# Block of gMLP, mLSTM and a squared-ReLU MLP on one core: the fetches of the second MLP product's row operands go out from GpSimd's queue instead of SyncE's

## The chip, the core and the metric

The kernel runs on one core of a Trainium2 chip. Five engines work side by side, each through its own instruction stream in order: TensorE (PE, matrix products; PEld is its loading of weights), VectorE (DVE), ScalarE (ACT), GpSimd (POOL) and SyncE (SP). Data move by DMA: an engine issues a transfer, goes on, and whoever needs the data waits on a semaphore. SP does nothing but issue transfers. An engine that has to wait before it may issue holds up everything behind that in its stream. The metric is the device time of one execution in microseconds (us).

## The reference, cut to what matters

One decoder block over 512 tokens of 2048 features, in float32. Two token mixers (a gated MLP with spatial gating and an mLSTM) come first; the part around the change is the MLP behind them and the last norm:

```python
        x = x + mixed @ w_out[l]
        hn = _rms_norm(x, norm2_g[l])
        x = x + jnp.square(jax.nn.relu(hn @ w_ff1[l])) @ w_ff2[l]
    return _rms_norm(x, norm_f_g)
```

`w_ff1` is 2048 x 8192, `w_ff2` 8192 x 2048. "First product" and "second product" below are those two.

## The kernel before, in words

**Precision and form of the products.** Every float32 operand is split into a rounded part hi (ScalarE, a cast) and a rest lo (DVE, a subtraction), and a product is made as three matmuls. The large products use a scheme with seven block products in place of eight: sums and differences of quarters, A11, A12, A22, S1, S2, S3 and S4, stand on both sides, so that operands have to be made from pieces before they can be multiplied.

**First product.** 32 column tiles. `hidden` (L945) applies the squared ReLU and writes each tile to the DRAM tensor `h_d` from POOL (L949).

**Second product.** The 8192 hidden features are worked through in NB = 4 blocks c of 2048, and each in two units, for the column halves j0 = 0 and 4 (`unit`, `token_unit`). A unit has 28 parts of 12 matmuls, four weight chunks for each of the seven operations, in the order A11/S1 in turns, S2/S4 in turns, S3, A12/A22 in turns. Each part needs a weight chunk (512 KB, fetched by SP at L1070 into `raw` or `raw2` buffers), differences of chunks (DVE, L59), and its hi (ACT, L1059) and lo (DVE, L1060). Results are drained from PSUM into tiles `o` (ACT L1160, DVE L1162), and written to the DRAM tensor `sum_d` from POOL (L1167): as plain writes for c = 0, and accumulating for c = 1 and 2. In the last block they come back the other way (L1196).

**The row operands.** What the weights of a unit multiply are the operands h of block c. `hidden_parts(c, ...)` makes them: for each of four groups g, four pieces of `h_d` are fetched by `hidden_piece` (L1020, 128 partitions x 2 x 256 floats, 256 KB each) into `tmp` tiles named hp, and A11, S1, S2 and S4 are made from them; then S3 for each g, from two pieces fetched again; then A12 and A22 for each g, one piece each. That is 32 fetches a block, 128 in all. Each operand costs one sum or difference on DVE (hp, L59; none for A11, A12, A22), a cast on ACT (L137) and a subtraction on DVE (h, L59). The pool `tmp` has four buffers, so a fetch waits until an earlier piece has been used. The operands fill 28 buffers, and a new block's operand waits until the old one in its place has been multiplied for the last time.

**Who runs when.** `hidden_parts` is a generator. `beside` registers it, and each part of a product calls `tick`, which lets every registered generator take one step. The generator for c = 0 starts two ticks into tile 30 of the first product, that for c + 1 in the second unit of block c, when 14 of its 28 parts are done. The framework's scheduler then sets the order on each engine from the order of the code, the dependencies and its own assumed durations, so that one engine's stream mixes both. The weights' hi and lo are held in the order of the parts (`in_turn`). Semaphores follow from the data.

In `before`, SP's stream carries the weight chunks and the fetches of pieces; POOL's carries the writes of `h_d` and `sum_d` and, at the end, of x3.

Of the kernel before, what the change touches and what calls it, by code (L numbers as in the profile page):

```python
# [17 lines left out]
S2 = S // 2  # L18
# [15 lines left out]
def hybrid_block(ctx: ExitStack, tc: tile.TileContext, a: dict, out: bass.AP):  # L34
    nc = tc.nc
# [7 lines left out]
    def t4k(name, dt=F32, shape=None):  # L43
        return sb.tile(shape or [P, 2, S], dt, tag="t4k", bufs=28, name=name)

    def tmp(name, shape=None, dt=F32):
        return sb.tile(shape or [P, S], dt, tag="tmp", bufs=4, name=name)
# [96 lines left out]
    def v2(t):  # L144
        return t.rearrange("p (e t) -> p e t", e=2)
# [641 lines left out]
    def fetch(src, name):  # L787
        t = tmp(name)
        nc.sync.dma_start(t, src)
        return t  # L790
# [67 lines left out]
    for i in range(8):  # L858
        t = t4k(f"mix_{i}")
# [11 lines left out]
    for g in range(4):  # L871
        q = [pair(f"mq_{g}_{kh}") for kh in range(2)]
        for e in range(2):
            for kh in range(2):
# [3 lines left out]
                t = fetch(sg_d[0][j], f"sga_{j}")  # L878
# [62 lines left out]
    h_d = dram.tile([P, DFF // P, S], F32, name="h_d")  # L941
# [78 lines left out]
    def hidden_piece(c, kh, th, g):  # L1020
        t = v2(tmp(f"hp_{c}_{kh}_{th}_{g}"))
        k = c * KT + kh * 8 + g * 2
        nc.sync.dma_start(t, h_d[:, k : k + 2, th * S2 : (th + 1) * S2])
        return t

    def hidden_parts(c, xo):

        for g in range(4):
            a11, a21 = hidden_piece(c, 0, 0, g), hidden_piece(c, 0, 1, g)
            a22, a12 = hidden_piece(c, 1, 1, g), hidden_piece(c, 1, 0, g)  # L1030
            put(xo, "A11", a11, f"h{c}_{g}")
            yield
            put(xo, "S1", tt(a22, a21, a22, ALU.add), f"h{c}_{g}")
            yield
            put(xo, "S2", tt(a22, a22, a11, ALU.subtract), f"h{c}_{g}")
            yield
            put(xo, "S4", tt(a12, a12, a22, ALU.subtract), f"h{c}_{g}")
            yield
        for g in range(4):
            a21, a11 = hidden_piece(c, 0, 1, g), hidden_piece(c, 0, 0, g)  # L1040
            put(xo, "S3", tt(a21, a11, a21, ALU.subtract), f"h{c}_{g}")
            yield
        for g in range(4):
            for op, th in (("A12", 0), ("A22", 1)):
                put(xo, op, hidden_piece(c, 1, th, g), f"h{c}_{g}")
            yield
# [342 lines left out]
```

## Time and profile before

| | before |
|---|---|
| median of 3 runs | 2541.51 us (2537.47 to 2547.2) |
| the profiled execution | 2543.25 us, span 2541.5 us |
| mean granted PE clock | 0.985 of full speed |
| transfers issued by SP (queue q1) | 318.29 MB, 40.3% of the DMA engines' time |
| transfers issued by POOL (queue q0) | 56.71 MB, 7.9% |

The span is the part of the execution in which the profile shows instructions. Times within it count from its start; the second product begins at about 1851 us, and its blocks turn at about 2015, 2177 and 2343 us. The granted clock is the share of TensorE's full speed that the chip allowed over a stretch; its two levels are 1.2 and 2.4 GHz.

### The profile page before, as it was taken

To read this page: it belongs to the slowest core of one execution; us is meant where nothing else is said; L and a number is where in the kernel's file an instruction comes from. 1 tells how busy PE (TensorE), PEld (TensorE's weight loads), DVE (VectorE), ACT (ScalarE), POOL (GpSimd) and SP (SyncE) were. 2 spreads that over 40 slices of the span, in tenths; PEclk is the share of its full clock that TensorE was granted. 3 is DMA by queue.
4 is the path that set the end of the run, shared out by engine and by line. 5 is a ranking of instruction groups with operands and counts; after the bars stand their busy time and mean duration, and the time that the engine had idled before them with its cause. 6 is when DMAs were issued, how large, how long until landed. Compare 5 with 4: busy or idle time off the path is not lost.

```text
span 2541.5 us, 34288 instructions
## 1 busy us (share of the span) xinstructions
PE 2462.9 (97%) x12810; PEld 2080.7 (82%) x12810; DVE 2078.7 (82%) x2852; ACT 1302.1 (51%) x1913; POOL 155.1 (6%) x242
## 2 busy tenths in 40 slices
PE   8999999999999999999999999999989999999996
PEld 7888888888887888888888888888868787787785
DVE  6988888888878756889788888888878878888787
ACT  6555464554455223555555555555654545544544
POOL 0001001001001000000000000000000010011000
PEclk9999999999999999999999999999999999999998
DMA  7323333333335644355344433443665776678564
GB/s 270 109 87 117 124 104 112 121 105 129 112 100 187 206 162 141 110 153 149 103 139 135 137 127 135 134 141 133 212 186 144 237 179 153 181 163 226 144 193 137
DMA packets 197366, 377.17 MB, mean 148 GB/s; under 512 B 14784, under 2 KB 124352, under 8 KB 197200
## 3 DMA queue, kind: packets, MB, share of 16 engines
q1 hardware_dynamic: 177552, 318.29, 40.3%
q0 software_dynamic: 19648, 56.71, 7.9%
q8 instruction: 100, 1.64, 0.3%
q14 instruction: 66, 0.54, 0.1%
HBM read 320.41 MB, written 54.53 MB: 148 GB/s over the span
## 4 chain that ended last, share of the span: by engine, by line
PE 76%; DVE 9%; issue 6%; DMA 6%; ACT 2%; POOL 1%; DVEq 0%; SPq 0%; POOLq 0%; ACTq 0%
PE pw_f_x L155 8%; DMA hp<-h_d 4%; PE pw_f_z L155 4%; PE pw_f_x L156 4%; PE pt_f_x L1092 3%; PE pt_f_x L1090 3%; PE pt_f_x L1091 3%; PE pw_g_x L155 3%; PE pw_f_z L156 2%; PE pw_f_y L155 2%; PE pt_f_z L1092 2%; PE pp_g L155 2%; PE pt_f_z L1090 2%; PE pt_f_z L1091 2%; PE pw_g_x L156 1%
## 5 line engine op out<-in xcount | busy, mean ns | idle before, releaser
L59 DVE TENSOR_TENSOR raw_f<-raw_f,raw_f 128x1024 f32<-128x1024 f32 x228 | 277.5, 1221 | 10.4 <-DMA raw_f<-in_w_ff 8.3
L126 DVE TENSOR_TENSOR lo_f_S<-raw_f,hi_f_S 128x1024 fp32r<-128x1024 f32 x116 | 141.8, 1223 | 44.6 <-ACT hi_f_S L125 44.6
L1059 ACT CAST hi_f_S<-raw_f 128x1024 fp32r<-128x1024 f32 x112 | 116.9, 1048 | 112.7 <-DVE raw_f L59 80.6
L155 PE MATMUL pw_f_z<-x_S,hi_f_S 128*128 128x512 f32 x448 | 163.1, 404 | 0.0
L125 ACT CAST hi_f_A<-raw_f 128x1024 fp32r<-128x1024 f32 x87 | 91.2, 1049 | 137.4 <-DVE raw_f L59 71.6
L155 PE MATMUL pw_f_x<-x_S,hi_f_S 128*128 128x512 f32 x448 | 159.9, 397 | 0.0
L1060 DVE TENSOR_TENSOR lo_f_S<-raw_f,hi_f_S 128x1024 fp32r<-128x1024 f32 x112 | 136.5, 1222 | 28.7 <-ACT hi_f_S L1059 28.2
L155 PE MATMUL pw_f_x<-x_A,hi_f_A 128*128 128x512 f32 x448 | 158.4, 396 | 0.0
L125 ACT CAST hi_f_S<-raw_f 128x1024 fp32r<-128x1024 f32 x116 | 121.2, 1046 | 57.5 <-DVE raw_f L59 30.2
L126 DVE TENSOR_TENSOR lo_f_A<-raw_f,hi_f_A 128x1024 fp32r<-128x1024 f32 x87 | 106.5, 1224 | 46.9 <-ACT hi_f_A L125 46.8
L1059 ACT CAST hi_f_A<-raw_f 128x1024 fp32r<-128x1024 f32 x84 | 87.6, 1046 | 81.4 <-DVE raw_f L59 61.3
L1060 DVE TENSOR_TENSOR lo_f_A<-raw_f,hi_f_A 128x1024 fp32r<-128x1024 f32 x84 | 101.7, 1222 | 33.1 <-ACT hi_f_A L1059 32.8
L156 PE MATMUL pw_f_z<-x_S,lo_f_S 128*128 128x256 f32 x448 | 125.8, 281 | 0.0
L156 PE MATMUL pw_f_x<-x_A,lo_f_A 128*128 128x256 f32 x448 | 125.3, 280 | 0.0
L156 PE MATMUL pw_f_x<-x_S,lo_f_S 128*128 128x256 f32 x448 | 125.3, 280 | 0.0
L1090 PE MATMUL pt_f_x<-hi_f_A,h_A 128*128 128x512 f32 x224 | 91.4, 408 | 17.1 <-ACT hi_f_A L1059 10.3
L155 PEld LDWEIGHTS pw_f_z<-x_S,hi_f_S 128*128 128x128 f32 x448 | 84.8, 189 | 22.8 <-DVE f L59 1.9
L155 PEld LDWEIGHTS pw_f_x<-x_S,hi_f_S 128*128 128x128 f32 x448 | 84.1, 188 | 20.8
L155 PEld LDWEIGHTS pw_f_x<-x_A,hi_f_A 128*128 128x128 f32 x448 | 84.1, 188 | 20.3
L155 PE MATMUL pp_g<-xu,hi_g 128*128 128x512 f32 x256 | 92.7, 406 | 8.1 <-ACT hi_g L125 7.8
L1090 PE MATMUL pt_f_z<-hi_f_S,h_S 128*128 128x512 f32 x224 | 89.3, 398 | 6.6 <-ACT hi_f_S L1059 6.6
L1092 PE MATMUL pt_f_x<-lo_f_A,h_A 128*128 128x512 f32 x224 | 91.3, 409 | 2.6 <-DVE lo_f_A L1060 2.5
(560 smaller groups left out, 7807.6 us busy)
## 6 DMA issues: line engine op xcount, KB each, us to landing
raw_f<-in_w_ff SPq DMA_DIRECT2D x240, 512.0 KB, 4.3
hp<-h_d SPq DMA_DIRECT2D x128, 256.0 KB, 4.2
raw_g<-in_w_gb SPq DMA_DIRECT2D x32, 512.0 KB, 3.9
raw_g<-in_w_ga SPq DMA_DIRECT2D x32, 512.0 KB, 3.3
raw_wout<-in_w_out SPq DMA_DIRECT2D x32, 512.0 KB, 3.3
h_d<-f POOLq DMA_DIRECT2D x60, 256.0 KB, 2.3
sum_d<-o POOLq DMA_DIRECT2D x48, 256.0 KB, 5.8
sg<-g POOLq DMA_DIRECT2D x32, 256.0 KB, 2.4
```

What stands on the lines that cost most here:

```text
L59: V.tensor_tensor(o, x, y, op=op)
L125: in_turn("A", A.copy(hi[:, c], src[:, c]))
L126: in_turn("V", V.tensor_tensor(lo[:, c], src[:, c], hi[:, c].bitcast(F32), op=ALU.subtract))
L155: T.matmul(ps, wh, x, start=first, stop=False, skip_group_check=more)
L156: T.matmul(ps[:, :S2], wl, x[:, :S2], start=False, stop=last, skip_group_check=more)
L1059: in_turn("A", A.copy(vh, v))
L1060: in_turn("V", V.tensor_tensor(vl, v, vh.bitcast(F32), op=ALU.subtract))
L1090: T.matmul(ps[t], xh, wh, start=b, stop=False, skip_group_check=not first)
L1091: T.matmul(ps[t], xl, wh, start=False, stop=False, skip_group_check=not first)
L1092: T.matmul(ps[t], xh, wl, start=False, stop=e, skip_group_check=not first)
```

## The change

One line: the fetch of a piece is issued by GpSimd instead of SyncE.

```diff
     def hidden_piece(c, kh, th, g):
         t = v2(tmp(f"hp_{c}_{kh}_{th}_{g}"))
         k = c * KT + kh * 8 + g * 2
-        nc.sync.dma_start(t, h_d[:, k : k + 2, th * S2 : (th + 1) * S2])
+        nc.gpsimd.dma_start(t, h_d[:, k : k + 2, th * S2 : (th + 1) * S2])
         return t
```

SP's stream goes from 709 rows to 581, POOL's from 240 to 368. The scheduler also sets other orders on ACT and DVE. In the rows below, hp_1_0_3 is the piece kh = 1, th = 0, g = 3 (the number of the block isn't printed), raw_f_0_0_3_0 is block 0, unit 0, quarter 3 of the weights, chunk 0, and operands show only the letter of their operation.

SP at the end of the first product, the difference between the kernel before and the changed one, from the fourth chunk of quarter 1 to the four chunks of quarter 0 with which the first part of the second product begins:

```order
 L1070 DMA raw_f_0_0_3_0_16983<-in_w_ff 128x4x256
-L1023 DMA hp_1_0_3_16750<-h_d 128x2x256
-L1023 DMA hp_0_1_0_16859<-h_d 128x2x256
-L1023 DMA hp_0_0_0_16861<-h_d 128x2x256
-L1023 DMA hp_0_1_1_16887<-h_d 128x2x256
-L1023 DMA hp_0_0_1_16889<-h_d 128x2x256
-L1023 DMA hp_0_1_2_16912<-h_d 128x2x256
-L1023 DMA hp_0_0_2_16914<-h_d 128x2x256
 L1070 DMA raw_f_0_0_0_0_16773<-in_w_ff 128x4x256
 L1070 DMA raw_f_0_0_0_1_16818<-in_w_ff 128x4x256
 L1070 DMA raw_f_0_0_0_2_16867<-in_w_ff 128x4x256
 L1070 DMA raw_f_0_0_0_3_16920<-in_w_ff 128x4x256
```

The seven fetches that stood between the two groups of chunks are gone from SP; the four chunks now follow the one ahead of them directly.

POOL in the turn from block 1 to block 2, of the changed kernel (before, POOL had only the `sum_d` rows here, one behind the other):

```order
L1167 DMA sum_d<-o_4_010_18911 128x512
L1167 DMA sum_d<-o_4_011_18913 128x512
L1023 DMA hp_0_1_3_19189<-h_d 128x2x256
L1023 DMA hp_1_1_3_19191<-h_d 128x2x256
L1023 DMA hp_1_0_3_19193<-h_d 128x2x256
L1023 DMA hp_0_1_0_19298<-h_d 128x2x256
L1167 DMA sum_d<-o_4_110_18769 128x512
L1167 DMA sum_d<-o_4_111_18771 128x512
L1023 DMA hp_0_0_0_19300<-h_d 128x2x256
L1023 DMA hp_0_1_1_19323<-h_d 128x2x256
```

The fetches for S1 of g = 3 (hp_0_1_3 and hp_1_1_3) stand behind the first two writes of sums, and one of the two fetches for the first S3 (hp_0_0_0) behind the next two.

DVE at the same place, the difference: the sum for S1 of g = 3 is the row hp_1_1_3 <- hp_0_1_3, hp_1_1_3, the additions into o are L1162, the operands of the last A12/A22 parts L1060:

```order
 L1060 TENSOR_TENSOR lo_f_1_4_A_0_19036<-raw_f_1_4_2_0_19033,hi_f_1_4_A_0_19035 128x1024
+L59 TENSOR_TENSOR raw_f_1_4_2_0_19033<-raw_f_1_4_2_0_19033,raw_f_1_4_0_0_18617 128x1024
 L59 TENSOR_TENSOR hp_1_1_3_19191<-hp_0_1_3_19189,hp_1_1_3_19191 128x512
-L59 TENSOR_TENSOR raw_f_1_4_2_0_19033<-raw_f_1_4_2_0_19033,raw_f_1_4_0_0_18617 128x1024
-L59 TENSOR_TENSOR h_3_S_19220<-hp_1_1_3_19191,h_3_S_19220 128x2x256
-L59 TENSOR_TENSOR hp_1_1_3_19191<-hp_1_1_3_19191,hp_0_0_3_19187 128x512
 L1162 SCALAR_TENSOR_TENSOR o_4_110_18769<-pt_f_1_4_x_18613,r2c,o_4_110_18769 128x512
 L1162 SCALAR_TENSOR_TENSOR o_4_111_18771<-pt_f_1_4_x_18614,r2c,o_4_111_18771 128x512
 L1060 TENSOR_TENSOR lo_f_1_4_A_0_19057<-raw_f_1_4_2_0_19033,hi_f_1_4_A_0_19056 128x1024
 L1060 TENSOR_TENSOR lo_f_1_4_A_1_19079<-raw_f_1_4_2_1_19076,hi_f_1_4_A_1_19078 128x1024
```

The weight difference raw_f_1_4_2_0 moved ahead of the sum, and the lo half of S1 (h_3_S) and the next difference moved behind the additions into o.

## Rows read from the trace of the kernel before

**Rows 1.** The page: busy time of each engine and two kinds of DMA issues.

```profile
PE 2462.9 (97%) x12810; PEld 2080.7 (82%) x12810; DVE 2078.7 (82%) x2852; ACT 1302.1 (51%) x1913; POOL 155.1 (6%) x242
...
hp<-h_d SPq DMA_DIRECT2D x128, 256.0 KB, 4.2
...
h_d<-f POOLq DMA_DIRECT2D x60, 256.0 KB, 2.3
```

**Rows 2.** Four stretches and a steady one: length, busy time (instructions) by engine, granted clock, DMA.

```profile
1840.00:1880.00 40.00, 28.11 (x111) 21.70 (x110) 32.52 (x40) 24.36 (x36) 1.08 (x2) 0.87 0.64 191
1920.00:1980.00 60.00, 60.00 (x264) 49.19 (x263) 53.58 (x56) 33.55 (x42) 3.13 (x6) 1.00 0.52 142
1980.00:2060.00 80.00, 76.25 (x319) 61.27 (x319) 69.21 (x75) 41.29 (x52) 3.35 (x7) 0.96 0.70 205
2140.00:2200.00 60.00, 52.60 (x207) 41.04 (x206) 49.13 (x57) 27.80 (x36) 6.59 (x8) 0.91 0.82 222
2300.00:2370.00 70.00, 62.45 (x247) 49.44 (x246) 57.89 (x67) 34.01 (x45) 6.91 (x8) 0.90 0.77 206
```

**Rows 3.** PE's waits, 1780 to 2430: waited for, us, times, longest.

```profile
PE pt_f_x L1090 <- ACT hi_f_A L1059: 10.3, 1, 10.3
PE pt_f_x L1090 <- DVE o L1162: 6.8, 3, 2.7
```

**Rows 4.** Timeline of SP, end of the first product: start, us from first to last.

```profile
1832.53 0.37 SPq L1070 DMA_DIRECT2D raw_f<-in_w_ff  x1
1833.13 11.28 SPq L1023 DMA_DIRECT2D hp<-h_d  x7
1844.50 2.47 SPq L1070 DMA_DIRECT2D raw_f<-in_w_ff  x4
```

**Rows 5.** The chain that ended last in 1795 to 1885: start, us, what.

```profile
1844.05 3.07 DMA hp<-h_d
...
1848.86 10.69 DMA hp<-h_d
```

**Rows 6.** Timeline of ACT, 1838 to 1862.

```profile
1846.71 0.35 ACT L162 COPY o_f<-pp_f 128x256 f32<-128x256 f32 x1
...
1850.32 1.04 ACT L1059 CAST hi_f_A<-raw_f 128x1024 fp32r<-128x1024 f32 x1 [1.11 <-DMA raw_f<-in_w_ff]
```

**Rows 7.** The chain in 2144 to 2158, between the second and third block.

```profile
2142.42 7.51 DMA hp<-h_d
...
2149.96 0.69 DVE hp L59
2150.65 1.14 DVE raw_f L59
2151.79 0.61 DVE h_S L59
...
2153.03 1.40 DVE o L1162 x2
```

**Rows 8.** The chain in 2177 to 2192, start of the third block.

```profile
2179.54 7.96 DMA hp<-h_d
...
2189.12 1.24 DVE lo_f_S L1060
```

**Rows 9.** Timeline of POOL, 2130 to 2200.

```profile
2139.69 1.72 POOL L1167 DMA_DIRECT2D sum_d<-o  x2 [43.20 <-DVE o L1162]
2154.07 1.72 POOL L1167 DMA_DIRECT2D sum_d<-o  x2 [12.65 <-DVE o L1162]
2176.61 2.60 POOL L1167 DMA_DIRECT2D sum_d<-o  x3 [20.81 <-DVE o L1162]
```

**Rows 10.** The issues of line 1167: ns min/median/max, then us from issue to landing.

```profile
L1167 POOL DMA_DIRECT2D sum_d<-o x48: 539/850/1408, 1900.7 to 2346.1; - x48
...
DMA to landing us min/median/max: 2.3/5.8/8.6
```

**Rows 11.** The issues of line 1023: ns min/median/max.

```profile
L1023 SPq DMA_DIRECT2D hp<-h_d x128: 359/360/1722, 1796.9 to 2360.4; - x128
```

## The prediction

> **What bounds the kernel now.** I began with the page: TensorE (PE) is busy for 97% of the span, VectorE (DVE) for 82%, and GpSimd (POOL) for only 6% [rows 1]. So only time in which PE stands still or runs slowly can be won, and POOL has room for more issues. The busy time by stretches shows where that time lies. In the steady stretch 264 matmuls take 60.00 us, 0.2273 us each, at full granted clock; in the other four the count of matmuls times 0.2273 us is less than the stretch [rows 2]. The differences are 14.8 us around the start of the second product (40 - 111 x 0.2273), 7.5 us at the turn from block 0 to block 1, 13.0 us from 1 to 2, and 13.9 us from 2 to 3: 49 us together. The granted clock there is 0.87 to 0.96 of 2.4 GHz, thus partly at the lower level of 1.2 GHz, because PE restarts slowly after each pause; that is in the 49 us. All four stretches are those in which the fetches of line 1023 run, so **49 us, 1.9%, is the most that this change can win**.
>
> PE's own waits name two sorts of cause: one wait of 10.3 us for the first rounded weight tile (hi, ScalarE, L1059), and three of together 6.8 us for DVE's additions into o [rows 3]. Next I read what stands ahead of each.
>
> *Start of the second product.* SP's timeline shows one weight chunk issued at 1832.53, then seven fetches over 11.28 us, and only at 1844.50 the four chunks with which the first part begins [rows 4]. A fetch has to wait for one of four tmp buffers, and the weights stand behind it in SP's queue. ScalarE rounds the first chunk at 1850.32, released by its arrival [rows 6]. The chain shows the fetch for the third S3 landing at 1847.12 and the one for the fourth S3 taking 10.69 us, against a median of 4.2 us, since 2 MB of weights were issued just ahead of it [rows 1, 5].
>
> *Turns between blocks.* In the turn from 1 to 2 a fetch issued at 2142.42 lands 7.51 us later, at 2149.93. DVE then does the sum of pieces (0.69 us), a weight difference (1.14 us), the lo half of S1 (0.61 us) and one more difference before the additions into o start at 2153.03; PE's next part waits for those [rows 3, 7]. At the start of block 2 a fetch issued at 2179.54 takes 7.96 us and holds up a cast, so that the lo part of S1's second chunk comes at 2189.12 [rows 8]. The other turns look alike.
>
> **The change, part by part.** The one edited line moves 128 issues from SP to POOL, and the order of ScalarE's and DVE's work follows from it.
>
> *The issue.* An issue on SP takes 0.36 us [rows 11]. No 128-partition fetch on POOL is in the trace; the nearest are the plain writes of the same 256 KB, at 0.54 us [rows 10], landing after a median of 2.3 us [rows 1]. I take 0.54 us and the old time to landing. The 128 issues then cost POOL 69 us on an engine that is 94% idle. Where fetches follow one another through the buffers it costs 0.18 us each. I see no reason why the first byte must come sooner or later; the bounds are 2.3 us (the write) and 7.96 us (the longest that held up a turn).
>
> *Start of the second product.* SP now has the four chunks right behind the one of 1832.53, some 11 us earlier, so they are there before ScalarE wants them (a flight took 5.8 us, 1844.50 to 1850.32). In the new order hi stands behind the cast of the second S3 and the copy at 1846.71 that ends at 1847.06 [rows 6], no longer behind the cast of the third S3. So it can start 3.3 us sooner. Its lo half still stands behind the sum of the third S3 on DVE, and that fetch (1847.12) ends a row of three that each pay 0.18 us and now share the DMA engines with 2 MB of weights. I take **-2 us**, of a possible -3.3, and 0 if the fetches lose as much as the weights gain. The fourth S3's fetch no longer stands behind those weights: with the median of 4.2 us it lands 6.5 us earlier. Of the 14.8 us some 4.5 us are not the one long wait; I take **-2 us** of these, at most -4.5.
>
> *Turns: DVE's order.* The weight difference now stands ahead of the sum that waits, and the lo half of S1 and the second difference behind the additions into o. With an unchanged landing the additions start 0.69 us after it, at 2150.65 instead of 2153.03: 2.4 us for each turn.
>
> *Turns: POOL's queue.* What takes it back is that a fetch now stands behind writes of sums. Those that stand just ahead of it were issued from 2139.69 to 2141.41, so the issue itself isn't held; but they are accumulating, with a median of 5.8 us to landing and up to 8.6 us [rows 9, 10]. They can be underway until 2149.2 (2140.55 + 8.6), with two fetches behind them, while the weights on SP's queue no longer stand ahead. I take a landing 1 us later than now; the bounds are 2 us earlier and 4 us later. In the turn from 0 to 1 the sums are plain writes (0.54 us to issue, 2.3 us at least to landing): no delay taken.
> Two other places are in the same queue. The fetch for the first S3 now stands behind the sums issued at 2154.07, which wait for DVE; before it came ahead of them. I take a new wait of 1 us (bounds 0 and 4) in each of the turns 1 to 2 and 2 to 3. The last fetch for the fourth S3 stands behind the three of 2176.61, so it goes out after 2179.2; with the 7.96 us of now it lands at 2187.2, and lo comes after a sum and a difference (0.69 + 1.14 us), at 2189.0, as now; with 5.8 us it gains 2 us. I take -1 us.
>
> So 0 to 1: -2.4 and a little of slow clock, **-3 us**. 1 to 2 and 2 to 3: -2.4 + 1 + 1 - 1 = -1.4, **-1.5 us** each.
>
> **The sum** is -2 - 2 - 3 - 1.5 - 1.5 = -10 us. The profiled execution took 2543.25 us, 1.7 us above the median of 2541.51; that gives 2533 against its own time and 2531.5 against the median. **2532 us** it is, -0.4%. A measurement of this kernel tells some 0.5% (12.7 us) from no change, so this is just inside.
>
> A rule speaks against part of the gain. The profile shows plain writes on POOL's queue landing in 2.3 us [rows 1] though SP's stream of weights runs beside them, so two queues do not simply line up behind one another. The Trainium skill (DMA: Bandwidth & Descriptors, Issuing engines are not separate DMA queues) says that transfers from all issuing engines share the same 16 engines, and that another issuing engine saves only the time of the issue. By that rule the weights' head start would be paid by the fetches, which gives the rival "no gain" below.
>
> **The rivals.**
> *No gain.* Bytes are the same, and the DMA engines are at 0.64 to 0.82 of their time in these stretches [rows 2]; the weights come early and the fetches as much later. Start: 0; turns: the 2.4 us are lost to landings 2.4 us later. About 2542 us. For it: the DMA shares. Against: at the start it was a wait for buffers, not the engines, that held the weights back.
> *All of it.* Fetches land in 2.3 to 3 us as in an empty queue; the four stretches lose only half. 25 us less: 2517 us. For it: the 2.3 us of the writes. Against: the sums ahead in the queue.
> *Slower.* Accumulating sums hold POOL's queue in order: a fetch lands only when both sums and its neighbour have, 13 us after the release. It decides from about 10 us, where the 2.4 us are used up. Then each of the three places of a turn is some 4 us late, in two turns: +24 us, with -8 us of the rest: +16 us, 2558 us. For it: the 8.6 us. Against: the median of 5.8 us.
> *Fetches wait for DVE.* If a fetch could start only when a DVE instruction ends, each on the path would come up to 1.2 us later: three at the start and three at each turn, 12 x 1.2 = +14, less 10: 2546 us. Against: the 2.3 us of POOL's writes beside a DVE at 82% [rows 1]. The Trainium skill (SBUF — State Buffer, the warning on "DVE blocks DMA") states such a block, for two-port modes of DVE.
>
> **How the numbers follow.** The forecast (-4 to -18 us) has 0.45, "all of it" 0.20, "no gain" 0.13, "slower" 0.17, "wait for DVE" 0.05. Of the forecast's 0.45 I put 0.18 beyond 12.7 us. Faster by over 0.5%: 0.18 + 0.20 = 0.38. Slower: 0.17. Within: 0.45. The range takes in the forecast and the nearer half of "all of it" and of "slower": from 2511 us to 2553 us; the forecast's own is 2524 to 2538 us.
>
> **What would show it.** Right: the four chunks issued before 1836 on SP; PE's 10.3 us wait down to 7 to 8 us; the fourth S3's fetch at 4 to 5 us; additions into o starting within 1 us of the fetch that they stand behind; fetches on POOL with 0.54 us an issue. Wrong: fetches beside weights at a median above 6 us; a wait of PE for lo of A22's third chunk above 3 us; fetches behind the sums that take over 10 us; the cast of h waiting for DMA at the blocks' start as long as before.

## The result and the profile after

Measured in turns on one chip, 8 runs of each: **2529.04 us (2525.2 to 2533.91) after, 2541.72 us (2537.47 to 2548.65) before, a ratio of 0.9948 with a 95% interval of 0.9935 to 0.9961**. That is 12.7 us less, just at the 0.5% that can be told from no change. The forecast was 2532 us, its own range 2524 to 2538 us. The time came out near it, but in part by luck: two of its steps were off, in opposite directions.

First the page of the kernel after (busy time by engine; DMA queues with packets, MB and share; issues with KB and the median us to landing):

```profile
span 2527.4 us, 34252 instructions
...
PE 2451.2 (97%) x12810; PEld 2073.7 (82%) x12810; DVE 2076.2 (82%) x2852; ACT 1300.6 (51%) x1913; POOL 248.5 (10%) x370
...
q1 hardware_dynamic: 142736, 284.73, 36.0%
q0 software_dynamic: 29888, 90.27, 12.3%
...
raw_f<-in_w_ff SPq DMA_DIRECT2D x240, 512.0 KB, 4.5
hp<-h_d POOLq DMA_DIRECT2D x128, 256.0 KB, 3.5
...
sum_d<-o POOLq DMA_DIRECT2D x48, 256.0 KB, 5.5
```

The 33.6 MB of fetches are now in q0 (90.27 against 56.71 MB). Their median to landing is 3.5 us, 4.2 us before [rows 1]. Next the same stretches as in [rows 2]: start of the second product, steady, and the turns 0 to 1, 1 to 2, 2 to 3.

```profile
1840.00:1880.00 40.00, 27.63 (x105) 21.52 (x106) 33.48 (x41) 24.05 (x36) 13.26 (x19) 0.79 0.59 178
1920.00:1980.00 60.00, 60.00 (x265) 49.30 (x264) 53.94 (x57) 33.26 (x42) 9.01 (x14) 1.00 0.53 145
1980.00:2060.00 80.00, 76.87 (x330) 62.53 (x329) 71.01 (x77) 41.91 (x54) 21.80 (x32) 0.98 0.72 209
2140.00:2200.00 60.00, 53.76 (x232) 42.61 (x231) 52.05 (x60) 32.01 (x42) 20.64 (x28) 1.00 0.81 217
2300.00:2370.00 70.00, 65.24 (x275) 51.96 (x274) 60.40 (x66) 35.13 (x45) 18.81 (x25) 0.98 0.74 195
```

Length less the count of matmuls times 0.2273 us gives what each stretch loses, as it did before:

| stretch | lost before | lost after | change | predicted |
|---|---|---|---|---|
| start of the second product | 14.8 | 16.1 | +1.3 | -4 |
| turn 0 to 1 | 7.5 | 5.0 | -2.5 | -3 |
| turn 1 to 2 | 13.0 | 7.3 | -5.7 | -1.5 |
| turn 2 to 3 | 13.9 | 7.5 | -6.4 | -1.5 |
| sum | 49.2 | 35.9 | -13.3 | -10 |

The sum is close to the 14.1 us by which the span shrank (2541.5 to 2527.4), so the gain lies in the four stretches. At the turns the granted clock went from 0.96, 0.91 and 0.90 to 0.98, 1.00 and 0.98; at the start from 0.87 to 0.79. PE's waits over the second product name what is left (us in total, times, longest):

```profile
PE pt_f_x L1090 <- ACT hi_f_A L1059: 12.7, 1, 12.7
PE pt_f_x L1092 <- DVE lo_f_A L1060: 8.1, 6, 2.3
PE pt_f_z L1092 <- DVE lo_f_S L1060: 4.9, 5, 1.4
PE pt_f_x L1090 <- DVE o L1162: 1.5, 3, 0.7
```

Against [rows 3] the wait for the first hi grew from 10.3 to 12.7 us, and the three for additions into o shrank from 6.8 to 1.5 us.

**The start.** SP's timeline after shows the chunk of 1832.53 and the four of 1844.50 [rows 4] now issued in one row:

```profile
1831.36 4.56 SPq L1070 DMA_DIRECT2D raw_f<-in_w_ff  x5
```

So the weights were there early. (The first of the five is, by its name in the listing of the change, the first chunk of quarter 3, not the fourth of quarter 1.) POOL's timeline holds the fetches, DVE's the sums that wait for them:

```profile
1832.23 0.71 POOL L1023 DMA_DIRECT2D hp<-h_d  x1 [1.10 <-DVE h_S L59]
1836.48 0.72 POOL L1023 DMA_DIRECT2D hp<-h_d  x1 [3.54 <-DVE hp L59]
1838.82 0.71 POOL L1023 DMA_DIRECT2D hp<-h_d  x1 [1.62 <-DVE hp L59]
```

```profile
1841.05 0.69 DVE L59 TENSOR_TENSOR hp<-hp,hp 128x512 f32<-128x512 f32 x1 [2.76 <-DMA hp<-h_d]
...
1845.33 0.69 DVE L59 TENSOR_TENSOR hp<-hp,hp 128x512 f32<-128x512 f32 x1 [2.21 <-DMA hp<-h_d]
...
1847.87 0.69 DVE L59 TENSOR_TENSOR hp<-hp,hp 128x512 f32<-128x512 f32 x1 [0.48 <-DMA hp<-h_d]
```

The first of these fetches landed after 8.7 us, the other two after 7.0 and 6.4 us, while the five chunks came in (they landed from 1836.8 to 1846.4). On the same queue the two fetches just ahead of the weights (1826.93 and 1829.28) and two behind them (1846.31 and 1847.69) took 3.0 to 3.3 us. Every one of these sums waited for its fetch, and each sum gives the next fetch its buffer. The sum of the second S3 is the one at 1847.87; before, it began at 1844.13, 3.7 us sooner. On ScalarE hi stands where the prediction put it, behind the cast of the second S3 and the copy:

```profile
1848.60 0.62 ACT L137 CAST h_S<-hp 128x512 fp32r<-128x512 f32 x1 [1.39 <-DVE hp L59]
...
1850.46 0.63 ACT L162 COPY o_f<-pp_f 128x256 f32<-128x256 f32 x2
1850.97 1.06 ACT L1059 CAST hi_f_A<-raw_f 128x1024 fp32r<-128x1024 f32 x1
```

That place came as much later as the new order had won: hi at 1850.97, against 1850.32 of [rows 6].

**The turn from 1 to 2.** DVE's timeline shows the order that the prediction read: the weight difference ahead of the sum that waits for a fetch, the additions into o right behind it.

```profile
2143.22 1.23 DVE L59 TENSOR_TENSOR raw_f<-raw_f,raw_f 128x1024 f32<-128x1024 f32 x1
2147.43 0.69 DVE L59 TENSOR_TENSOR hp<-hp,hp 128x512 f32<-128x512 f32 x1 [2.98 <-DMA hp<-h_d]
2148.03 1.40 DVE L1162 SCALAR_TENSOR_TENSOR o<-pt_f_x,r2c,o 128x512 f32<-128x512 f32 x2
...
2162.23 0.69 DVE L59 TENSOR_TENSOR hp<-hp,hp 128x512 f32<-128x512 f32 x1 [2.85 <-DMA hp<-h_d]
```

On POOL, the fetch for the sum of 2147.43, two sums of blocks, and the fetch for the sum of 2162.23, with the last one's flight in the chain:

```profile
2141.15 1.46 POOL L1023 DMA_DIRECT2D hp<-h_d  x2 [1.45 <-DVE h_S L59]
...
2149.13 1.83 POOL L1167 DMA_DIRECT2D sum_d<-o  x2
2154.61 0.76 POOL L1023 DMA_DIRECT2D hp<-h_d  x1 [3.65 <-ACT hi_f_A L1059]
```

```profile
2154.61 7.53 DMA hp<-h_d
```

The first fetch has landed 6.3 us after its issue (2147.43 - 2141.15) where it took 7.51 us [rows 7], and the additions begin 0.6 us after the sum does. The second stands behind accumulating sums, takes 7.53 us, and holds DVE for 2.85 us. That is the new wait: PE stands for lo of A22's third chunk, up to 2.3 us at a time.

**The start of block 2.** ScalarE's timeline:

```profile
2179.39 1.05 ACT L1059 CAST hi_f_S<-raw_f 128x1024 fp32r<-128x1024 f32 x1 [3.28 <-DVE raw_f L59]
...
2182.70 1.28 ACT L137 CAST h_A<-hp 128x512 fp32r<-128x512 f32 x2 [0.60 <-DMA hp<-h_d]
```

A cast of h waits for DMA 0.60 us, and hi of the weights now goes ahead of it. In [rows 8] a fetch of 7.96 us stood ahead there. By the gaps between matmuls (start to start, less the 0.2273 us) PE lost 1.6 us in S1's second chunk at this turn, 4.6 us before, and 1.6 instead of 6.0 us at the next.

### The profile page after: what moved, and what is told of

It reads as the page before. It is cut to its first block, busy times and chain, and to the rows that moved or that the text cites. A ratio compares the mean times of both kernels' runs of the same rounds, so it can differ in the third digit from the quotient of the medians.

```text
span 2527.4 us, 34252 instructions
## 1 busy us (share of the span) xinstructions
PE 2451.2 (97%) x12810; PEld 2073.7 (82%) x12810; DVE 2076.2 (82%) x2852; ACT 1300.6 (51%) x1913; POOL 248.5 (10%) x370
## 3 DMA queue, kind: packets, MB, share of 16 engines
q1 hardware_dynamic: 142736, 284.73, 36.0%
q0 software_dynamic: 29888, 90.27, 12.3%
## 4 chain that ended last, share of the span: by engine, by line
PE 73%; DVE 10%; issue 8%; DMA 6%; ACT 2%; POOL 1%; DVEq 0%; SPq 0%; POOLq 0%; ACTq 0%
PE pw_f_x L155 8%; PE pw_f_z L155 4%; PE pw_f_x L156 4%; DMA hp<-h_d 3%; PE pt_f_x L1092 3%; PE pt_f_x L1090 3%; PE pt_f_x L1091 3%; PE pw_g_x L155 3%; PE pw_f_z L156 2%; PE pw_f_y L155 2%; PE pp_g L155 2%; PE pt_f_z L1092 2%; PE pt_f_z L1090 1%; PE pt_f_z L1091 1%; PE pw_g_x L156 1%
## 5 line engine op out<-in xcount | busy, mean ns | idle before, releaser
L59 DVE TENSOR_TENSOR raw_f<-raw_f,raw_f 128x1024 f32<-128x1024 f32 x228 | 277.1, 1221 | 10.3 <-DMA raw_f<-in_w_ff 8.4
L1060 DVE TENSOR_TENSOR lo_f_S<-raw_f,hi_f_S 128x1024 fp32r<-128x1024 f32 x112 | 135.8, 1221 | 18.6 <-ACT hi_f_S L1059 18.0
L1060 DVE TENSOR_TENSOR lo_f_A<-raw_f,hi_f_A 128x1024 fp32r<-128x1024 f32 x84 | 101.2, 1221 | 29.1 <-ACT hi_f_A L1059 29.1
L1023 POOL DMA_DIRECT2D hp<-h_d x128 | 93.1, 728 | 291.5 <-DVE hp L59 114.2
L1090 PE MATMUL pt_f_x<-hi_f_A,h_A 128*128 128x512 f32 x224 | 89.9, 401 | 14.2 <-ACT hi_f_A L1059 12.7
```

The source lines that it names most:

```text
L59: V.tensor_tensor(o, x, y, op=op)
L1023: nc.gpsimd.dma_start(t, h_d[:, k : k + 2, th * S2 : (th + 1) * S2])
L1060: in_turn("V", V.tensor_tensor(vl, v, vh.bitcast(F32), op=ALU.subtract))
L1090: T.matmul(ps[t], xh, wh, start=b, stop=False, skip_group_check=not first)
```

## The experiments

Two questions were open. At the turns: does the gain come from the queue (fetches off SP's stream) or from the order of VectorE's and ScalarE's work, which the one edited line also changed? At the start: why is there no gain, though the weights came early? The rival there was that four weight chunks ahead of need take the fetches' place in the DMA engines; another was that the S3, A12 and A22 operands stand in the way of hi at all. All ratios are against the kernel before, 4 to 11 runs of each in turns with it on one chip. The experiments ran in three groups, each on another chip, and the medians of the kernel before were 2543.26, 2542.65 and 2543.28 us there. For the stretches the table takes the same difference as above, over windows wide enough for kernels whose turns come earlier (1835:1900, 1960:2070, 2120:2220, 2280:2385).

| kernel | us | ratio (95%) | start | 0 to 1 | 1 to 2 | 2 to 3 |
|---|---|---|---|---|---|---|
| before | 2541.72 | 1 | 13.2 | 7.5 | 13.2 | 13.9 |
| after | 2529.04 | 0.9948 (0.9935 to 0.9961) | 15.0 | 5.0 | 7.3 | 7.5 |
| after, again | 2532.78 | 0.9957 (0.9944 to 0.9971) | 14.5 | 2.9 | 6.6 | 7.5 |
| turns only | 2528.56 | 0.9937 (0.9924 to 0.9951) | 13.9 | 3.6 | 7.5 | 8.2 |
| start only | 2547.32 | 1.0017 (1.0007 to 1.0027) | 15.7 | 7.9 | 12.0 | 15.7 |
| order alone | 2531.93 | 0.9950 (0.9936 to 0.9964) | 12.9 | 5.0 | 8.9 | 10.4 |
| order, more of it | 2531.93 | 0.9956 (0.9944 to 0.9968) | 14.5 | 6.6 | 8.4 | 7.5 |
| queue alone | 2542.07 | 0.9999 (0.9991 to 1.0008) | 13.2 | 7.3 | 11.8 | 13.9 |
| S3 later at the start | 2534.15 | 0.9961 (0.9948 to 0.9975) | 18.9 | 3.9 | 10.7 | 7.3 |
| plain sums | 2521.36 | 0.9914 (0.9902 to 0.9926) | 13.9 | 3.9 | 3.9 | 2.7 |
| first chunk first | 2526.78 | 0.9944 (0.9931 to 0.9957) | 7.7 | 7.0 | 7.7 | 7.3 |
| turns and first chunk | 2522.38 | 0.9920 (0.9907 to 0.9934) | 7.7 | 2.9 | 7.0 | 6.8 |
| and sums behind S3 | 2517.75 | 0.9903 (0.9889 to 0.9916) | 9.5 | 3.6 | 4.3 | 5.2 |

A stretch is from one profiled execution; the kernel after, profiled twice, differs by up to 2.1 us in one of them (turn 0 to 1), so smaller differences are not read.

### Half of the change each

Fetches of blocks 1 to 3 on GpSimd, those of block 0 (the start) on SyncE:

```diff
-        nc.gpsimd.dma_start(t, h_d[:, k : k + 2, th * S2 : (th + 1) * S2])
+        (nc.gpsimd if c else nc.sync).dma_start(t, h_d[:, k : k + 2, th * S2 : (th + 1) * S2])
```

> Fetches of blocks 1 to 3 on GpSimd's queue, those of block 0 back on SyncE's. Theory A (the whole gain comes at the turns between blocks; at the start of the second product the weights' head start is paid by later fetches): as fast as the changed kernel or up to 2 us faster, 2527 to 2530 us, with PE's first wait back at some 10 us. Theory B (the start gives a third of the gain, as the sum of the prediction has it): 2533 us.

And the other half:

```diff
-        nc.gpsimd.dma_start(t, h_d[:, k : k + 2, th * S2 : (th + 1) * S2])
+        (nc.sync if c else nc.gpsimd).dma_start(t, h_d[:, k : k + 2, th * S2 : (th + 1) * S2])
```

> Fetches of block 0 alone on GpSimd's queue. Theory A (nothing comes from the start): 2540 to 2544 us, no change from the kernel before. Theory B (the start gives 4 us): 2537 to 2538 us.

The turns alone gave 14.7 us (2543.26 to 2528.56), as much as the whole change or more; the start alone cost 4.1 us, its interval wholly above 1. PE's waits with the start alone:

```profile
PE pt_f_x L1090 <- ACT hi_f_A L1059: 13.9, 1, 13.9
PE pt_f_x L1090 <- DVE o L1162: 7.4, 3, 3.0
```

The first hi comes later, and the waits for o are nearly those of [rows 3]. Ahead of the second product's first matmul PE stands for 10.3 us before, 10.9 us with the turns only, 12.7 and 12.9 us in the two executions of the kernel after, and 13.9 us with the start only. (The times at which that matmul begins can't be compared: already 400 matmuls earlier, ahead of the first fetch, the executions lie between 1773.0 and 1778.4 us.) So the gain is the turns', and the fetches of block 0 on GpSimd have a cost.

### The order with the old queue, the queue with the old order

All fetches on SyncE, but the few instructions that the change had moved held in their new places. `held_back(x, key)` tells the scheduler that x comes after a marked instruction of the same engine; it puts no semaphore between them.

```diff
+        nc.sync.dma_start(t, h_d[:, k : k + 2, th * S2 : (th + 1) * S2])
...
+            s1 = vt(a22, a21, a22, ALU.add, *([("t4", u, 0)] if last else []))
+            put_at("S1", s1, f"h{c}_{g}", (), [("lo", f"{u}_A12_1")] if last else [])
...
+            s2 = vt(a22, a22, a11, ALU.subtract, *([("t4", u, 1)] if last else []))
...
+            put_at("S3", s3, f"h{c}_{g}", [("hi", f"{w}_A11_2")] if g == 3 and c else [])
...
+                put_at(op, hidden_piece(c, 1, th, g), f"h{c}_{g}", [("hi", f"{w}_A11_2")] if g == 0 and c else [])
```

Here "t4" marks the weight difference of a chunk in A22, "lo" and "hi" the halves of a chunk; `u` is the unit that ends, `w` the one that begins, `last` the fourth group.

> All fetches on SyncE's queue as before, but at the turns the sums and operands on VectorE and ScalarE are held to nearly the order of the changed kernel (weight difference ahead of the sum for S1 of the last group, lo of S1 and the next difference behind the additions into o, the casts of the last S3 and first A12 and A22 behind the hi of the third A11 chunk). Theory C (the gain is the order's): 2529 to 2533 us with PE's waits for o below 1 us each. Theory D (the gain is the queue's: fetches no longer behind weights): 2539 to 2543 us, since the sum still waits for a fetch of 6.5 to 7.5 us. Half and half: 2535 us.

The order alone gave 11.3 us, 0.9950, with not one fetch moved to another queue. SyncE's own stream was not held: at each turn a few rows of it changed places, among them a fetch that now goes out behind a weight chunk. The waits:

```profile
PE pt_f_z L1127 <- DVE lo_f_S L1093: 10.1, 4, 3.8
PE pt_f_x L1127 <- DVE lo_f_A L1093: 3.2, 3, 1.7
PE pt_f_x L1125 <- DVE o L1198: 3.0, 2, 1.7
```

The waits for o are down, from 6.8 to 3.0 us (1.5 in the kernel after; one of 1.7 us is above what Theory C allowed). New is that PE waits up to 3.8 us for lo of S1's first chunk at a block's start, behind sums for S3 that stand ahead on DVE and wait for their fetch. By the gaps between matmuls that chunk lost 4.6, 5.3 and 5.9 us, 1.0 to 1.6 us before. So I held the S3 operands of the later groups back too:

```diff
+            first = {0: ("t4", u, 2), 3: ("lo", f"{w}_A11_1")}.get(g)
+            s3 = vt(a21, a11, a21, ALU.subtract, *([first] if first and c else []))
+            then = {1: ("lo", f"{w}_A11_0"), 2: ("lo", f"{w}_A11_1")}.get(g)
```

> As the run with the order alone (all fetches on SyncE), and the sums and lo of S3 of the later groups are held behind the lo of the first parts of the next block too. In that run these stood ahead of lo of the first S1 chunk, which cost PE 4.6 to 5.9 us at each turn. Theory C: 4 us less at each turn, 2518 to 2524 us, faster than the changed kernel without GpSimd's queue. Rival: the fetch is late whatever stands ahead, and the wait comes one part later: 2529 to 2533 us.

No further gain can be told (2531.93 us again, and the four stretches lose 37.0 us together, 37.2 with the order alone): PE still lost 2.4 to 3.7 us in S1's first chunk, and 1.4 to 2.4 us in S2's second, where before it had lost nothing. The rival that the wait would only change its place was right.

The reverse, fetches of blocks 1 to 3 on GpSimd with the instructions held nearly where they stood before the change (`ahead_of` is `held_back` the other way round):

```diff
+        (nc.gpsimd if c else nc.sync).dma_start(t, h_d[:, k : k + 2, th * S2 : (th + 1) * S2])
...
+            s1 = vt(a22, a21, a22, ALU.add, *([("t4", u, 0)] if last else []))
+            put_at("S1", s1, f"h{c}_{g}", (), [("o", u)] if last else [])
...
+            s2 = vt(a22, a22, a11, ALU.subtract, *([("o", u)] if last else []))
```

> Fetches of blocks 1 to 3 on GpSimd's queue, but at the turns VectorE and ScalarE held to nearly the order of the kernel before (the sum for S1 of the last group ahead of the weight difference, lo of S1 ahead of the additions into o, the casts of the last S3 and the first A12 and A22 ahead of the hi of the second S1 chunk). Theory C (the gain is the order's): 2541 to 2547 us, no gain, PE's waits for o above 2 us again. Theory D (the gain is the queue's): 2528 to 2532 us.

It made no difference: 0.9999 (0.9991 to 1.0008).

```profile
PE pt_f_x L1133 <- ACT hi_f_A L1099: 18.9, 4, 10.5
```

Beside the first wait of 10.5 us three of together 8.4 us stand at the turns, where [rows 3] had 6.8 us. They are put down to ScalarE's hi of A22's first chunk and not to o, but the place is the same: by the gaps between matmuls A22's first chunk lost 4.9, 6.0 and 5.1 us at the three turns, 5.1, 6.1 and 5.8 us before, and 1.7, 2.2 and 3.2 us after. In the turn from 1 to 2 DVE's rows show the old order:

```profile
2147.81 0.69 DVE L1048 TENSOR_TENSOR hp<-hp,hp 128x512 f32<-128x512 f32 x1 [4.40 <-DMA hp<-h_d]
...
2150.89 1.40 DVE L1206 SCALAR_TENSOR_TENSOR o<-pt_f_x,r2c,o 128x512 f32<-128x512 f32 x2
```

The additions into o begin 3.1 us after the sum that waits for the fetch, as before (2149.96 and 2153.03 in [rows 7]), where the kernel after needs 0.6 us and the order alone 1.7 us. The two kernels settle the first question: **the new order of DVE's and ScalarE's work, not the queue, makes the gain at the turns**. Whether the queue adds a little once the order is there (0.9937 against 0.9950) can't be told, since the intervals overlap. This agrees with what the prediction weighed from the Trainium skill (DMA: Bandwidth & Descriptors, Issuing engines are not separate DMA queues), that another issuing engine saves only issue time: the queue alone moved the time by 0.6 us of 2542.65.

### The start

S3, A12 and A22 of block 0 made later, beside the first unit's parts instead of ahead of them, each behind the weights' hi and lo of its part:

```diff
-    beside(after(2, hidden_parts(0, hc)))
+    beside(after(2, hidden_parts(0, hc, (0,))))
...
+                if n == 1 and not j0 and not c:
+                    beside(hidden_parts(0, hc, (1,)))
```

> As the changed kernel, but S3, A12 and A22 of block 0 are made only from the second part of the second product on, each behind the hi and lo of its part. Theory E (what holds the first hi and lo is the row of casts and sums for S3, each behind its fetch): the first wait of PE falls from 12.7 us to 5 to 7 us and the kernel takes 2522 to 2525 us. Theory F (VectorE is full in the first parts and the waits only move there): 2528 to 2531 us.

The first wait fell by 5 us, but the stretch lost more than before, 18.9 us. PE's waits:

```profile
PE pt_f_x L1105 <- DVE lo_f_A L1073: 8.9, 7, 3.1
PE pt_f_x L1103 <- ACT hi_f_A L1072: 8.8, 2, 7.7
```

The work is given back within the first unit: it must be done there in any case, and DVE has no room for it beside the weights (it is busy for 34.3 of the 39 us from 1846 to 1885). The time, 0.9961, is not better than that of the kernel after.

The next kernel stands on the order held above, with all fetches on SyncE, and asks that the first weight chunk go ahead of the fetches for S3, A12 and A22; where the other three go is left to the scheduler:

```diff
+        if c == 0:
+            held_back(ins, "first")
...
+            if name == "f2_0_0" and q == 0 and kc == 0:
+                marks["first"] = ins
```

> As the run with more of the order held (all fetches on SyncE), and the fetches for S3, A12 and A22 of block 0 stand behind the first weight chunk of the second product on SyncE's queue. Theory E: hi and lo of the first part no longer stand behind the sums for S3, PE's first wait falls from 10.8 to 5 to 7 us, 4 us faster than without. Theory F: the wait moves to the S1 parts behind it, no change, or slower by up to 5 us as in the run that made S3 later.

PE's first wait was 4.0 us (10.3 before, 12.7 after), and the start lost 7.7 us instead of 13.2. It was not one chunk that went early. SyncE's timeline has three of them ahead of or among the fetches for S3:

```profile
1833.14 1.41 SPq L1109 DMA_DIRECT2D raw_f<-in_w_ff  x2
1834.66 2.25 SPq L1033 DMA_DIRECT2D hp<-h_d  x2
1836.95 1.43 SPq L1109 DMA_DIRECT2D raw_f<-in_w_ff  x1
```

The two fetches at 1834.66 took 7.3 and 8.5 us, no less than those of the kernel after. What the rule changed with the chunk's place is the order on ScalarE and DVE, where hi and lo now stand ahead of every operand of S3:

```profile
1843.96 1.06 ACT L1095 CAST hi_f_A<-raw_f 128x1024 fp32r<-128x1024 f32 x1
```

```profile
1847.45 0.69 DVE L1042 TENSOR_TENSOR hp<-hp,hp 128x512 f32<-128x512 f32 x1
```

The first is hi, the second the sum of the first S3, behind lo (1845.05); in the kernel after hi stood behind the cast of the second S3. So the wait fell as Theory E has it: hi and lo no longer stand behind work that waits for late fetches. Whether fewer chunks ahead are of use is not shown: no run sends only one. In the median it gained 5.2 us on the kernel without that rule (2531.93 to 2526.78), whose interval its own overlaps (0.9931 to 0.9957 against 0.9944 to 0.9968); PE lost about 2 us more in later chunks.

### The sums in POOL's queue

The kernel "turns only", with every sum of blocks written plainly instead of added to what is in DRAM. The sums over blocks are left out; the bytes and the queue stay.

```diff
-                more = {"accum_op": ALU.add} if c else {}
+                more = {}
```

> As the run with only blocks 1 to 3 on GpSimd, but the writes of sums of blocks 1 and 2 are plain instead of accumulating, so that the sums of the first three blocks aren't added up. Theory G (the new wait at A22's third chunk is that of a fetch behind accumulating writes in the same queue): the 3.5 and 4.1 us there fall to below 1 us as in the first turn, 2521 to 2525 us. Theory H (it comes from the second difference, which now stands later and frees the buffer later): no change, 2527 to 2530 us.

It took 2521.36 us, 7.2 us less than with the sums added (6.6 us by what each won against the kernel before on its own chip), and the intervals (0.9902 to 0.9926 and 0.9924 to 0.9951) nearly exclude each other. The turns 1 to 2 and 2 to 3, the two with accumulating sums, lost 3.9 and 2.7 us instead of 7.5 and 8.2; turn 0 to 1, whose sums are plain in either kernel, did not move (3.6 and 3.9). PE's wait for lo of A's chunks:

```profile
PE pt_f_x L1092 <- DVE lo_f_A L1060: 5.1, 7, 1.0
```

The longest is 1.0 us, 2.7 us with the sums added. By the gaps between matmuls A22's third chunk lost 1.1 and 0.7 us there, 3.5 and 4.1 us with the sums added. That alone would not do, for in other executions the same lateness is paid at A22's first chunk. But both together lost 3.2 and 2.4 us with plain sums, 5.5 and 6.4 us in this kernel with the sums added, and 4.3 to 4.8 us in three more executions (after, after again, turns and first chunk). So at these two turns the accumulation costs. Whether by what stands ahead of the fetch in the queue or by what the accumulating writes take of the DMA engines, this run does not tell. Nor did a run write the sums plainly with the fetches on SyncE, so how much of it the kernel before would win too stays open.

### A version that beats both

The kernel after once more, for comparison on the same chip:

> The changed kernel itself, beside the two below on one chip. All theories: a ratio of 0.994 to 0.996 to the kernel before.

It gave 0.9957, a first wait of 12.9 us, and waits for lo of A's chunks of at most 1.0 us: the wait at A22's third chunk isn't as long in every execution.

Turns only, with the rule of the first chunk:

```diff
+        ins = (nc.gpsimd if c else nc.sync).dma_start(t, h_d[:, k : k + 2, th * S2 : (th + 1) * S2])
+        if c == 0:
+            held_back(ins, "first")
```

> As the run with only blocks 1 to 3 on GpSimd, and the fetches for S3, A12 and A22 of block 0 on SyncE stand behind the first weight chunk of the second product. Theory E (the first wait of PE falls from 10.9 to 4 us, of which 2 us come back in the S2 and S1 parts of that unit, as in the run with the first chunk first): 2523 to 2527 us, ratio 0.992. Theory F: 2528 to 2530 us.

And with the last two sums of a unit (the writes of (1,1)) issued behind the second fetch for the first S3, which they had stood ahead of:

```diff
+        elif (c, kh, th, g) == (c, 0, 0, 0):
+            fetched[c] = fetched.get(c, 0) + 1
+            if fetched[c] == 2:
+                for late in sums_of.get(c - 1, ()):
+                    marks["s3"] = ins
+                    held_back(late, "s3")
```

> As that one, and on GpSimd's queue the two writes of sums that stood ahead of the second fetch for the first S3 now stand behind it, in all three turns, accumulating as before. Theory G (that fetch is late by the accumulating writes ahead of it): the 3.5 and 4.1 us at A22's third chunk fall to 1 to 2 us, 4 to 5 us faster than without, 2519 to 2523 us. Rival: the writes and the weights take the DMA engines wherever they stand, so the wait stays: no change.

They took 2522.38 and 2517.75 us. PE's waits in the last:

```profile
PE pt_f_x L1112 <- ACT hi_f_A L1079: 5.2, 1, 5.2
...
PE pt_f_x L1114 <- DVE lo_f_A L1080: 4.7, 6, 1.0
PE pt_f_x L1112 <- DVE o L1184: 0.4, 1, 0.4
```

Of the 25.5 us won against the kernel before, by the table 3.7 lie at the start, 3.9 in the turn 0 to 1, 8.9 in 1 to 2 and 8.7 in 2 to 3: 25.2 us. A22's first and third chunk together lost 4.7 and 4.4 us in the turns 1 to 2 and 2 to 3 of the first of these two kernels and 2.5 and 3.0 us in the second, with the sums accumulating in both; so the place in the queue seems to be a good part of what they cost. The step from the one to the other (4.6 us in the median) is not sure, as their intervals overlap; that both are faster than the kernels before and after is (the kernel after on the same chip: 0.9944 to 0.9971).

## Why the prediction was near, and where its steps failed

**The start, -4 us: wrong in sign.** The order on ScalarE was read rightly, and the chunks came before 1836 as predicted. The step that failed is "-2 us of a possible -3.3, and 0 if the fetches lose as much as the weights gain": they lost more. The place behind which hi stands came 3.7 us later, since its fetches flew 6.4 to 8.7 us beside the weights, and each issue cost 0.72 us, not 0.54. The half of the change shows the cost. The kernels with the rule of the first chunk show that it is the place of hi that counts: their fetches fly as long (7.3 to 9.0 us), but hi doesn't stand behind them, and the first wait is 4.0 to 5.2 us. That the weights' transfers slowed the fetches is read from the trace only (3.0 to 3.3 us just before and after them); no run held the weights back with the fetches on GpSimd. Of the second -2 us, half at most came: the fetch for the fourth S3 took 3.99 us instead of 10.69 us [rows 5], and what the stretch loses beside the one wait went from 4.5 us (14.8 - 10.3) to 3.4 us (16.1 - 12.7), which is less than two executions of one kernel can differ by. The chain shows that fetch:

```profile
1850.24 3.99 DMA hp<-h_d
```

**Turn 0 to 1, -3 us: right** (-2.5 us, and -4.6 us in the second execution of the kernel after).

**Turns 1 to 2 and 2 to 3, -1.5 us each: right in mechanism, too small.** -5.7 and -6.4 us came. The -2.4 us for DVE's order held: the additions into o start about 0.7 us after the landing, and the order alone brought the gain. Two terms were mis-sized. "A landing 1 us later" was 1.2 us shorter, 6.3 against 7.51 us, so the sums underway did not delay the fetch that DVE waited for; the one ahead of it, right behind the sums (2138.95), took 7.03 us. The "-1 us" for the fourth S3 and S1's second chunk was -3 and -4.4 us (4.6 and 6.0 us to 1.6), because in the new order the cast that waits for a fetch stands behind hi of the weights, which I had not counted: I had priced only the fetch's landing. With the queue alone and the old order S1's second chunk lost 4.7 and 4.3 us at these turns. The new wait of 1 us behind the sums exists, with a bound of 4; by the gaps between matmuls PE lost 3.8, 2.6 and 1.1 us there at the three turns of one execution, and 0.6, 0.9 and 0.9 us in the other, which lost 3.8 and 3.7 us at A22's first chunk in the later two turns instead of 2.2 and 3.2. The same lateness can thus be paid at either place. Why the first of the three, with plain sums, lost 3.8 us in one execution stays open.

**The rivals.** "No gain" fell by the intervals. It had the start right, where the weights' head start was paid by the fetches. "All of it" (2517 us) was not reached by this change; the last kernel took 2517.75 us and lost half of what the four stretches had lost, but by other edits, not by fetches that land in 2.3 to 3 us. "Slower" needed fetches held some 10 us behind the sums; the one there took 7.53 us. "Fetches wait for DVE" has little for it: with DVE busy for 82% the fetches' median went down, from 4.2 to 3.5 us, and the shortest took 3.0 us instead of 2.6, about as much more as the issue itself takes. The signs given for right and wrong divide in the same way. As predicted came the four chunks before 1836, the additions, the fourth S3's fetch, and a cast of h that waits less for DMA at a block's start. Against it stand the first wait, up instead of down, an issue of 0.72 us, and, at the start, fetches of 6.4 to 8.7 us beside the weights. No single wait for lo of A22's third chunk was above 3 us, though the chunk lost 3.8 us at one turn.

## What to carry to other kernels

An edit of a DMA's queue also changes what the scheduler puts where; hold the order by hand with the old queue, and the queue with the old order, before the queue is given the credit. In an in-order stream, work whose input comes late (a cast that waits for a fetch) belongs behind what the next engine waits for, and so does a transfer that isn't urgent (a sum of blocks). A head start for many transfers is paid by those beside them. When a total agrees with a forecast, compare stretch by stretch: here -13.3 against -10 us hid an error of 5 us in one place and another of 9 us in two others.

## What the hardware showed beyond that

A fetch issued from POOL costs more than a write of the same size from there, 0.54 us [rows 10], and about twice the 0.36 us on SP [rows 11] (count, then ns least, median and most):

```profile
L1023 POOL DMA_DIRECT2D hp<-h_d x128: 707/718/1048, 1795.1 to 2353.8; - x128
```

The fetches are cut differently by the two queues: q1 lost 34816 packets (177552 to 142736) and q0 gained 10240 (19648 to 29888) for the same 128 fetches, 272 against 80 each. The fastest landing was 2.6 us from SP and 3.0 us from POOL. Accumulating writes cost POOL more than plain ones: the issue of the sums in the kernel after, and then in the one with plain sums, whose landing follows.

```profile
L1167 POOL DMA_DIRECT2D sum_d<-o x48: 542/883/1447, 1900.4 to 2336.0; - x48
```

```profile
L1167 POOL DMA_DIRECT2D sum_d<-o x48: 540/557/585, 1900.0 to 2328.3; - x48
...
DMA to landing us min/median/max: 2.3/4.6/6.4
```

The median issue is 0.88 us against 0.56 us, over all 48, of which 16 are plain there too. With sums added the median to landing is 5.5 us on the page above, and POOL's longest issue 1.45 us.
